# One queue to another: state-space tables issued by GpSimd, signed powers and a fourth raw weight buffer in a two-layer decoder trunk

## The chip, the core and the metric

The kernel runs on one core of one Trainium2 chip. The metric is device time in microseconds of one execution. A profiled execution also leaves a trace of every instruction on the five engines: TensorE (PE in the profile, its weight loads PEld), VectorE (DVE), ScalarE (ACT), GpSimd (POOL) and SyncE (SP), which here only issues DMAs. An engine runs its instructions in a fixed order: one that waits holds up all behind it. SPq and POOLq are the DMA issues of SyncE and GpSimd.

## The reference

An input x of 512 rows by 1024 passes through two layers, each x + norm(mixer(norm(x))), all in fp32. Layer 0 has two parallel branches, of which the first is the state-space layer that the change is about:

```python
# layer 0
p = u @ ev_w_in            # 1024 -> 5 x 1024: a_in, a_z, b_val, b_gate, b_z
lam_bar = exp(lam * dt)    # 64 groups, 64 complex states each
b_bar   = ((lam_bar - 1) / lam) * B
s_t     = lam_bar * s_{t-1} + b_bar @ u_t       # 16 channels per group
ya      = Re(C @ s_t) + D * u_t
ya      = glu(gelu(ya)) * silu(a_z)
yb      = pointwise(swish(layer_norm(conv31(b_val * sigmoid(b_gate))))) * silu(b_z)
x       = x + norm(concat(ya, yb) @ ev_w_out)
# layer 1: chunked gated linear attention, 4 heads, then out projection
```

## The kernel before

**Weights.** Every weight is cut into blocks of 128x1024 and used in the order of `wlist` (line 85): blocks 0 to 7 project to the state-space input, then four for each of eight channel blocks c (value, gate and two gates for the end), then the later layers. A block is loaded by SyncE into a raw tile (`w_raw`, line 113; three buffers `wraw`). fp32 products are made of a rounded high half and the remainder: ScalarE casts the high half `wh` (line 143). For most blocks the low half `wl` is made by ScalarE writing -raw, rounded, into `wl` (line 130) and a DMA issued by GpSimd that adds raw onto it (line 131); for the others VectorE subtracts (line 149). `mm_st` (line 181) then does 16 matmuls with the high half (lines 186, 187) and 8 with the low half (line 189).

**State-space parameters.** `s5_params` (line 308) computes on VectorE, on tiles of 128x64, the phase of lam_bar, the powers `pr` (eight powers and a one, real and imaginary), and `prb` (the powers times (lam_bar-1)/lam). GpSimd computes `wb`, powers of the unit phase (lines 416 to 424). These use scratch pools `s5w` and `nat0`, which are closed at lines 463 and 464, after which the pools `q5` and `h5` are opened on the same side of the memory.

**State-space blocks.** For each of eight blocks of eight groups, `s5_prep(c)` (line 513) loads the coefficients `cb` (line 519, two buffers). ScalarE makes a signed copy of C's real part in `csp` (line 522) and the negation of its imaginary part in `ci` (line 523). Outer products with the powers (`outer`, line 525) give `bmt`, on VectorE for c below 2 and on GpSimd after, and `cme`, on VectorE. TensorE transposes `bmt` (line 544) and multiplies it with `csp` (line 551); ScalarE copies that to `ks` (line 554), TensorE transposes `ks` (line 555), and VectorE adds D into `kt` (line 557). `kt` goes to a DRAM table padded with zeros, `kt_d`, and comes back as `tm` (lines 563, 565). `phases` (line 492) multiplies two levels of `wb` on GpSimd to the cosine and sine tables of a pair of blocks, and SyncE copies them to `ct` and `st` in four DMAs a block (line 573). `s5_in(c)` (line 579) does the input side and the scan, `s5_out(c)` (line 619) the output side: its first step multiplies `tm` and `cme` (line 628) and copies to `ys`, its second transposes and applies GELU.

**The main loop** (line 703) writes for each block c: the two steps of `s5_in(c+1)`, the five of `s5_prep(c+2)` and the two of `s5_out(c)`, interleaved by hand, then the value and gate projections with the convolution (`value_gate`, line 668; the convolution's 30 steps of line 655 have low priority), then two more projections (`gate_z`). After the loop come the half-GLU (line 734), the output projection's first half, the layer norm over channels (line 759), the pointwise projection and the rest.

**Order.** The program is written for a framework that plans the order itself (`schedule_with_timeline_sim=True`, line 1213): it puts each engine's instructions in an order by a model of their times, from priorities (`feed` raises, `background` lowers them) and from when a buffer comes free. The order in the text of the program is therefore not the order on an engine. PSUM tiles come from three rings of banks: `mm` (3), `cv` (2) and `aux` (3).

Of the kernel before, what the change touches and what calls it, by code (L numbers as in the profile page):

```python
# [9 lines left out]
F32 = mybir.dt.float32  # L10
# [3 lines left out]
ALU = mybir.AluOpType  # L14
# [3 lines left out]
P = 128  # L18
D = 1024
S = 512  # L20
KT = D // P
# [3 lines left out]
NG = 64  # L25
GP = 16
NS = 64
GC = P // GP
NB = 64
DVE_PREP = 2  # L30
TB = S // NB
# [20 lines left out]
def trunk(ctx: ExitStack, tc: tile.TileContext, A: dict, out: bass.AP, dbg: dict | None = None):  # L52
    nc = tc.nc
    V, G, SC, PE, SY = nc.vector, nc.gpsimd, nc.scalar, nc.tensor, nc.sync
# [4 lines left out]
    wpool = ctx.enter_context(tc.tile_pool(name="wpool", bufs=2, side="left"))  # L59
# [20 lines left out]
    sgn = const.tile([P, 1], F32, name="sgn")  # L80
# [32 lines left out]
    def w_raw():  # L113
        i = wst["next_raw"]
        if i >= len(wlist):
            return
        raw = wpool.tile([P, 1024], F32, tag="wraw", bufs=3, name=f"wraw{i}")
        SY.dma_start(raw, wlist[i])
        wst["raw"][i] = raw
        wst["next_raw"] = i + 1  # L120
# [147 lines left out]
    wb = s5p.tile([P, 2, 2, NG // 2, 8], F32, name="wb")  # L268
    decay = s5p.tile([P, NG], F32, name="decay")
    dg = s5p.tile([P, NG, GP], F32, name="dg")  # L270
    SW = ExitStack()
    sw = SW.enter_context(tc.tile_pool(name="s5w", bufs=1, side="right"))
    par = sw.tile([P, 3, NG], F32, name="s5par")
# [14 lines left out]
    SY.dma_start(dd, bass.AP(tensor=sd.tensor, offset=sd.offset, ap=[[NG, GP], [0, TB], [1, NG]]))  # L288
    w_raw()
    SY.dma_start(cw, A["conv_w"])  # L290

    tps = [ps("mm") for _ in range(3)] + [ps("cv") for _ in range(2)] + [ps("aux") for _ in range(3)]
    for tt in range(TT):
# [14 lines left out]
    def s5_params():  # L308
# [74 lines left out]
        tt_(t1, cp_, sq, ALU.mult)  # L383
        tt_(s1, s1, t1, ALU.add)


        V.memset(pr[:, 0, :, 8], 1.0)
        V.memset(pr[:, 1, :, 8], 0.0)
        V.tensor_tensor(out=pr[:, :, :, 7], in0=ph[:, :, :, 0], in1=e.unsqueeze(1).to_broadcast([P, 2, NG]), op=ALU.mult)

        scr = {V: [sw.tile([P, 2, NG, 4], F32, name=f"s5u{i}") for i in range(2)],
               G: [ya[:, i, 0:S // 2].rearrange("p (w g m) -> p w g m", w=2, m=4) for i in range(2)]}

        def cmul(eng, o, a, b):

            sh = list(a.shape)
            u, w = (x[:, :, :, :sh[3]] for x in scr[eng])
            eng.tensor_tensor(out=u, in0=a, in1=b[:, 0].unsqueeze(1).to_broadcast(sh), op=ALU.mult)
            eng.tensor_tensor(out=w, in0=a, in1=b[:, 1].unsqueeze(1).to_broadcast(sh), op=ALU.mult)
            eng.tensor_tensor(out=o[:, 0], in0=u[:, 0], in1=w[:, 1], op=ALU.subtract)  # L400
            eng.tensor_tensor(out=o[:, 1], in0=u[:, 1], in1=w[:, 0], op=ALU.add)

        for m in (1, 2, 4):
            lo = 8 - m
            cmul(V, pr[:, :, :, lo - m:lo], pr[:, :, :, lo:8], pr[:, :, :, lo:lo + 1])
# [3 lines left out]
        tt_(e2, e, e, ALU.mult)  # L409
        tt_(e2, e2, e2, ALU.mult)  # L410
        tt_(decay, e2, e2, ALU.mult)
        phs, ph2, ph4 = (sw.tile([P, 2, NG // 2, 1], F32, name=f"s5ph{i}") for i in (1, 2, 4))
        for a, rows in enumerate((slice(0, NS), slice(NS, P))):
            V.tensor_copy(phs[rows].rearrange("p w (i g) o -> p w i (g o)", g=GC),
                          ph[rows].rearrange("p w (i a g) o -> p w i a (g o)", a=2, g=GC)[:, :, :, a, :])
        cmul(G, ph2, phs, phs)
        cmul(G, ph4, ph2, ph2)
        for lvl in range(2):
            G.memset(wb[:, lvl, 0, :, 0], 1.0)
            G.memset(wb[:, lvl, 1, :, 0], 0.0)  # L420
# [32 lines left out]
        for o, (f0, f1, op) in enumerate(((cr, ci, ALU.subtract), (cis, crs, ALU.add))):  # L453
            V.tensor_tensor(out=prb[:, o], in0=pr[:, 0, :, 1:9], in1=bc(f0), op=ALU.mult)
            V.tensor_tensor(out=pt, in0=pr[:, 1, :, 1:9], in1=bc(f1), op=ALU.mult)
            V.tensor_tensor(out=prb[:, o], in0=prb[:, o], in1=pt, op=op)

        G.memset(md, 0.0)
        G.affine_select(out=md, in_=md, pattern=[[-TB, GP]], compare_op=ALU.not_equal, fill=1.0, base=1 - TB, channel_multiplier=1)
        G.tensor_tensor(out=dg, in0=md.unsqueeze(1).to_broadcast([P, NG, GP]), in1=dd.unsqueeze(2).to_broadcast([P, NG, GP]), op=ALU.mult)  # L460
# [2 lines left out]
    NP.close()  # L463
    SW.close()
    q5 = S5.enter_context(tc.tile_pool(name="q5", bufs=1, side="right", reuse_waits="tile"))
    h5 = S5.enter_context(tc.tile_pool(name="h5", bufs=2, side="right", reuse_waits="tile"))

    dump("u0h", uh.bitcast(F32))


    u_d = [dram.tile([P, TB, NB], F32, name=f"u_d{c}") for c in range(KT)]

    kt_d = [dram.tile([GP, 2 * TB - 1, P], F32, name=f"kt_d{i}") for i in range(2)]
    zt = q5.tile([P, (TB - 1) * P // TB], F32, name="zt")
    G.memset(zt, 0.0)
    for t in kt_d:
        SY.dma_start(t[:, TB:2 * TB - 1].rearrange("p s n -> p (s n)").rearrange("p (a b) -> p a b", a=TB), zt)

    csps = [q5.tile([P, GC, 32], F32, name=f"csp{i}") for i in range(2)]
    for t in csps:  # L480
        G.memset(t[:, :, GP:32], 0.0)

    svs = [q5.tile([P, GC, NB], F32, name=f"sv{i}") for i in range(2)]
    rv = q5.tile([P, GC, NB], F32, name="rv")
    for t in svs + [rv]:
        G.memset(t[:, :, 0:1], 0.0)

    prep = {}

    pair = {}  # L490

    def phases(c):

        sh = [P, GC, 8, 8]
        ws = slice(c // 2 * GC, c // 2 * GC + GC)

        def w1(w):
            return wb[:, 1, w, ws, :].unsqueeze(3).to_broadcast(sh)

        def w0(w):  # L500
            return wb[:, 0, w, ws, :].unsqueeze(2).to_broadcast(sh)

        out_ = []
        for o, (a, b, op) in enumerate(((0, 1, ALU.subtract), (1, 0, ALU.add))):
            r_ = h5.tile(sh, F32, tag=f"ph{o}", bufs=1, name=f"ph{o}_{c}")
            wt = h5.tile(sh, F32, tag="wt", bufs=1, name=f"wt{o}_{c}")
            G.tensor_tensor(out=r_, in0=w1(0), in1=w0(a), op=ALU.mult)
            G.tensor_tensor(out=wt, in0=w1(1), in1=w0(b), op=ALU.mult)
            G.tensor_tensor(out=r_, in0=r_, in1=wt, op=op)
            out_.append(r_.rearrange("p g a b -> p (g a b)"))  # L510
        pair[c // 2] = out_

    def s5_prep(c):

# [1 line left out]
        pe_ = V if c < DVE_PREP else G  # L516
        gs = slice(g0_, g0_ + GC)
        cb = h5.tile([P, 4, GC, GP], F32, tag="cb", bufs=2, name=f"cb{c}")
        SY.dma_start(cb, A["s5cb"][c])
        cr_ = csps[c % 2]  # L520
        ci_ = h5.tile([P, GC, GP], F32, tag="ci", bufs=1, name=f"ci{c}")
        SC.activation(cr_[:, :, 0:GP], cb[:, 0], AF.Copy, scale=sgn)
        SC.mul(ci_, cb[:, 1], -1.0)

        def outer(eng, o, pt, h, pw, m1, m2, pa):
            sh = list(o.shape)
# [5 lines left out]
            eng.tensor_tensor(out=o, in0=o, in1=pt, op=ALU.add)  # L532

        bm = q5.tile([P, GC, P], F32, tag="bm", bufs=2, name=f"bm{c}")
        cme = q5.tile([P, GC, TB, GP], F32, tag="cme", bufs=3, name=f"cme{c}")
        kt = q5.tile([P, GC, GP], F32, tag="kt", bufs=2, name=f"kt{c}")
        for h in range(2):
            hs = slice(h * 4, h * 4 + 4)
            bmt = q5.tile([P, 4, GP, TB], F32, tag="bmt", bufs=2, name=f"bmt{c}")
            pt1 = h5.tile([P, 4, GP, TB], F32, tag="wt", bufs=1, name=f"pt1_{c}")  # L540
            outer(pe_, bmt, pt1, h, prb, cb[:, 2, hs], cb[:, 3, hs], 2)
            tp = ps("aux")
            for j in range(4):
                PE.transpose(tp[:, j * P:(j + 1) * P], bmt[:, j].rearrange("p q s -> p (q s)"), ident)
            with feed():
                SC.copy(bm[:, hs, :], tp.rearrange("p (g n) -> p g n", n=P))
            yield

            kp = ps("aux")
            for j in range(4):  # L550
                PE.matmul(kp[32 * j:32 * j + 32, 0:P], cr_[:, h * 4 + j, :], bmt[:, j].rearrange("p q s -> p (q s)"), start=True, stop=True)
            ks = q5.tile([P, P], F32, tag="ks", bufs=2, name=f"ks{c}")
            with feed():
                SC.copy(ks, kp[:, 0:P])
            PE.transpose(kp[:, P:2 * P], ks, ident)
            with feed():
                V.tensor_tensor(out=kt[:, hs, :], in0=kp[:, P:2 * P].rearrange("p (g q) -> p g q", q=32)[:, :, 0:GP],
                                in1=dg[:, g0_ + h * 4:g0_ + h * 4 + 4, :], op=ALU.add)
            pt2 = q5.tile([P, 4, TB, GP], F32, tag="pt", bufs=1, name=f"pt2_{c}")
            outer(V, cme[:, hs], pt2, h, pr, cr_[:, hs, 0:GP], ci_[:, hs], 3)  # L560
            yield
        kd = kt_d[c % 2]
        SY.dma_start(kd[:, 0:TB], kt.rearrange("p g q -> p (g q)"))
# [3 lines left out]
        if c % 2 == 0:  # L567
            phases(c)
        half = slice(c % 2 * NS, c % 2 * NS + NS)
        ct_, st_ = (h5.tile([P, S], F32, tag=n, bufs=2, name=f"{n}{c}") for n in ("ct", "st"))  # L570
        for dst, src in zip((ct_, st_), pair[c // 2]):
            for r_ in range(2):
                SY.dma_start(dst[r_ * NS:r_ * NS + NS], src[half])
        prep[c] = (bm, cme, tm, ct_, st_)
        yield

# [119 lines left out]
    def run(g, n=1):  # L696
        for _ in range(n):
            next(g)
# [4 lines left out]
    for c in range(KT):  # L703
        nx = s5_in(c + 1) if c + 1 < KT else iter([None] * 2)
        pre = s5_prep(c + 2) if c + 2 < KT else iter([None] * 5)
        cur = s5_out(c)
        run(nx)
        run(pre, 2)
        run(nx)
        run(cur)  # L710
        run(pre, 2)
        run(cur)
        run(pre)
        value_gate(c)
        gate_z(zb_d[c])
        gate_z(za_d[c])
# [500 lines left out]
```

## Time and profile before

| | us |
|---|---|
| median of 3 runs | 946.44 |
| lowest, highest | 945.23, 946.85 |
| the profiled execution | 946.38 |
| its span, first to last instruction | 944.7 |
| TensorE busy | 897.7 |
| VectorE busy | 641.9 |
| ScalarE busy | 485.1 |
| GpSimd busy | 245.4 |
| mean granted TensorE clock | 0.981 of full |

In a row of a timeline stand the start and the length in us, the engine, the line, the operation, the output and the inputs; in brackets, the idle time of the engine before it and what ended that. Rows of one kind that follow each other are merged (x4). In the list of waits stand the waiting and the releasing instruction, the us in total, the number of waits and the longest. In a row of a group stand the busy us, the mean ns of one, and the idle us ahead of them. In a row of DMA issues stand the KB of each and the median us from issue to landing.

### The profile page before, as it was taken

The page shows a single profiled execution, that of the slowest core. Times are in us where ns is not written, and L with a number is a line of the kernel's source. Part 1 is how long each engine was busy: PE and PEld are TensorE (multiplying, and loading weights), DVE is VectorE, ACT ScalarE, POOL GpSimd, SP SyncE. Part 2 cuts the span into 40 slices and gives each one's busy share as a digit, 9 for nine tenths or more (in the row PEclk, how much of TensorE's full clock was granted, in tenths as well). Part 3 has the DMA queues.
Part 4 walks back from the last instruction along what each step waited for, and adds up shares of the span by engine and source line. Part 5 has one row for each costly group of instructions (what it writes and reads, how often), then busy time and mean ns, then how long its engine had stood idle before and what let it go on. Part 6 is the DMA issues. An engine that isn't in the chain of part 4 may idle for free. (4 is left out here: it accounts for less than half of the span.)

```text
span 944.7 us, 12134 instructions
## 1 busy us (share of the span) xinstructions
PE 897.7 (95%) x4396; PEld 718.9 (76%) x4396; DVE 641.9 (68%) x1206; ACT 485.1 (51%) x693; POOL 245.4 (26%) x258
## 2 busy tenths in 40 slices
PE   5995998999999999999999979999999999999996
PEld 4873776777778877778887758888888888888875
DVE  7953999999989989832579477584483232744546
ACT  6542786786678855564444566343543242523430
POOL 2693657463123422011054002000200020000222
PEclk8998999999999999999999979999999999999998
DMA  9877987787988885288463112212212223324412
GB/s 278 228 198 194 229 199 184 178 205 204 215 220 228 210 231 179 92 224 201 153 215 124 45 63 93 84 37 82 90 67 90 73 83 135 134 89 164 193 45 89
DMA packets 54955, 142.74 MB, mean 151 GB/s; under 512 B 14256, under 2 KB 15792, under 8 KB 54896
## 3 DMA queue, kind: packets, MB, share of 16 engines
q1 hardware_dynamic: 46832, 112.62, 35.9%
q0 software_dynamic: 8064, 29.36, 17.3%
q8 instruction: 34, 0.56, 0.2%
q14 instruction: 25, 0.20, 0.1%
HBM read 95.18 MB, written 13.22 MB: 115 GB/s over the span
## 5 line engine op out<-in xcount | busy, mean ns | idle before, releaser
L143 ACT CAST wh<-wraw 128x1024 fp32r<-128x1024 f32 x126 | 132.1, 1048 | 161.4 <-PE ps_mm L801 92.5
L149 DVE TENSOR_TENSOR wl<-wraw,wh 128x1024 fp32r<-128x1024 f32 x70 | 87.0, 1243 | 115.2 <-ACT wh L143 114.8
L655 DVE SCALAR_TENSOR_TENSOR ps_cv<-h,cw,ps_cv 128x512 f32<-128x512 f32 x232 | 161.7, 745 | 2.7 <-ACT ps_cv L652 1.8
L186 PE MATMUL ps_mm<-u0h,wh 128*128 128x512 f32 x320 | 129.9, 407 | 1.0 <-ACT tmp L679 0.7
L187 PE MATMUL ps_mm<-u0l,wh 128*128 128x512 f32 x320 | 129.4, 405 | 0.0
L800 PE MATMUL ps_mm<-wh,u1h 128*128 128x512 f32 x240 | 96.2, 402 | 3.5 <-ACT wh L143 3.4
L801 PE MATMUL ps_mm<-wh,u1l 128*128 128x512 f32 x240 | 96.3, 401 | 0.8 <-DVE u1l L194 0.8
L131 POOL DMA_DIRECT2D wl<-wraw x56 | 48.9, 884 | 182.4 <-ACT wl L130 178.2
L802 PE MATMUL ps_mm<-wl,u1h 128*128 128x512 f32 x240 | 91.6, 401 | 1.6 <-DVE wl L149 1.6
L189 PE MATMUL ps_mm<-u0h,wl 128*128 128x512 f32 x320 | 82.5, 395 | 1.1 <-DMA wl<-wraw 1.1
L186 PEld LDWEIGHTS ps_mm<-u0h,wh 128*128 128x128 f32 x320 | 61.8, 193 | 16.4 <-issue 1.6
L130 ACT ACTIVATE wl<-wraw 128x1024 fp32r<-128x1024 f32 x56 | 59.2, 1057 | 25.8 <-DMA wraw<-in_w_in_dram 14.0
L187 PEld LDWEIGHTS ps_mm<-u0l,wh 128*128 128x128 f32 x320 | 61.7, 193 | 13.9 <-issue 1.1
L189 PEld LDWEIGHTS ps_mm<-u0h,wl 128*128 128x128 f32 x320 | 59.4, 188 | 14.9 <-DMA wl<-wraw 1.5
L800 PEld LDWEIGHTS ps_mm<-wh,u1h 128*128 128x128 f32 x240 | 45.9, 191 | 14.9 <-ACT wh L143 3.8
L971 POOL TENSOR_TENSOR rg<-rg,ng 128x512 f32<-128x512 f32 x16 | 24.2, 1544 | 124.6 <-ACT rg L970 124.6
L802 PEld LDWEIGHTS ps_mm<-wl,u1h 128*128 128x128 f32 x240 | 45.6, 191 | 13.1 <-DVE wl L149 2.3
L801 PEld LDWEIGHTS ps_mm<-wh,u1l 128*128 128x128 f32 x240 | 45.9, 191 | 11.7 <-DVE u1l L194 1.2
L186 PE MATMUL ps_mm<-u1h,wh 128*128 128x512 f32 x128 | 50.7, 396 | 0.0
L187 PE MATMUL ps_mm<-u1l,wh 128*128 128x512 f32 x128 | 50.5, 394 | 0.0
L1062 POOL TENSOR_TENSOR kr<-kr,fac 128x384 f32<-128x384 f32 x8 | 6.7, 837 | 124.2 <-DVE rr L205 65.1
L800 PE MATMUL ps_mm<-wh,oth 128*128 128x512 f32 x96 | 37.8, 396 | 0.5 <-ACT wh L143 0.5
(341 smaller groups left out, 1993.6 us busy)
## 6 DMA issues: line engine op xcount, KB each, us to landing
wl<-wraw POOLq DMA_DIRECT2D x56, 512.0 KB, 6.1
wraw<-in_w_in_dram SPq DMA_DIRECT2D x40, 512.0 KB, 5.2
wraw<-in_w_out_dram SPq DMA_DIRECT2D x32, 512.0 KB, 3.3
wraw<-in_w_vr_dram SPq DMA_DIRECT2D x32, 512.0 KB, 3.2
wraw<-in_w_qk_dram SPq DMA_DIRECT2D x16, 512.0 KB, 3.3
tm<-kt_d SPq DMA_DIRECT2D x8, 512.0 KB, 6.3
wraw<-in_w_glu_dram SPq DMA_DIRECT2D x8, 512.0 KB, 5.8
wraw<-in_w_pw_dram SPq DMA_DIRECT2D x8, 512.0 KB, 5.1
```

The lines of the kernel that those rows point to most:

```text
L130: SC.activation(l, raw, AF.Copy, scale=-1.0)
L131: G.dma_start(l.bitcast(F32), raw, accum_op=ALU.add)
L143: SC.copy(h, raw)
L149: V.tensor_tensor(out=l, in0=raw, in1=h.bitcast(F32), op=ALU.subtract)
L186: PE.matmul(acc, whv[:, k, :], xh[:, k, :], start=(k == 0), stop=False)
L187: PE.matmul(acc, whv[:, k, :], xl[:, k, :], start=False, stop=False)
L189: PE.matmul(acc, wlv[:, k, :], xh[:, k, :], start=False, stop=(k == KT - 1))
L655: V.scalar_tensor_tensor(out=acc, in0=h[:, k:k + S], scalar=cw[:, c, k:k + 1], in1=acc, op0=ALU.mult, op1=ALU.add)
L800: PE.matmul(accs[tt], xh[:, kt, ts_], whj, start=(first and j == 0), stop=False)
L801: PE.matmul(accs[tt], xl[:, kt, ts_], whj, start=False, stop=False)
L802: PE.matmul(accs[tt], xh[:, kt, ts_], wlj, start=False, stop=(last and j == 1))
L971: G.tensor_tensor(out=r_, in0=r_, in1=ng, op=ALU.mult)
```

## The change

- *Signed powers.* After `prb` is made, the powers `pr` are multiplied in place, the real part by the sign column `sgn`, the imaginary part by -1. `cme` is then made from `cb` directly, and the tile `ci` and line 523 are gone. `csp` stays for the matmuls.
- *Queues.* The cosine and sine tables share a tile `cs`, copied in two DMAs a block in place of four, issued by GpSimd in place of SyncE. The loads of `cb` for c of 2 and more are issued by GpSimd too.
- *Fourth raw buffer.* Of the first 36 blocks, those with i % 4 == 3 are loaded into a tile of the pool `q5` with one buffer of its own.
- *Zero-fills first.* The zeros for `kt_d`, `csp`, `sv` and `rv` are written ahead of the parameters, in tiles of the pool `s5p`; the zero tile `zt` is filled by VectorE instead of GpSimd; the two DMAs of zeros stand behind the load of the convolution's weights.
- *Early squares.* `phs`, `ph2` and `ph4` stand ahead of the powers in the program.
- *Order and buffers.* The first step of `s5_out(c)` stands first in its round and the second step moves up; `cme` has two buffers in place of three, `bmt` three in place of two.

```diff
@@ w_raw
-        raw = wpool.tile([P, 1024], F32, tag="wraw", bufs=3, name=f"wraw{i}")
+        if i < 36 and i % 4 == 3:
+            raw = wst["pool"].tile([P, 1024], F32, tag="wraw", bufs=1, name=f"wraw{i}")
+        else:
+            raw = wpool.tile([P, 1024], F32, tag="wraw", bufs=3, name=f"wraw{i}")
         SY.dma_start(raw, wlist[i])
@@ ahead of the parameters, in s5p instead of q5
+    zt = s5p.tile([P, (TB - 1) * P // TB], F32, name="zt")
+    V.memset(zt, 0.0)
+    csps = [s5p.tile([P, GC, 32], F32, name=f"csp{i}") for i in range(2)]
+    for t in csps:
+        G.memset(t[:, :, GP:32], 0.0)
+    svs = [s5p.tile([P, GC, NB], F32, name=f"sv{i}") for i in range(2)]
+    rv = s5p.tile([P, GC, NB], F32, name="rv")
+    for t in svs + [rv]:
+        G.memset(t[:, :, 0:1], 0.0)
...
     SY.dma_start(cw, A["conv_w"])
+    for t in kt_d:
+        SY.dma_start(t[:, TB:2 * TB - 1].rearrange("p s n -> p (s n)").rearrange("p (a b) -> p a b", a=TB), zt)
@@ s5_params: phs, ph2, ph4 now stand ahead of the powers; after prb:
+        V.tensor_scalar(out=pr[:, 0], in0=pr[:, 0], scalar1=sgn, scalar2=None, op0=ALU.mult)
+        V.tensor_scalar(out=pr[:, 1], in0=pr[:, 1], scalar1=-1.0, scalar2=None, op0=ALU.mult)
@@ phases
-            r_ = h5.tile(sh, F32, tag=f"ph{o}", bufs=1, name=f"ph{o}_{c}")
+        cs = h5.tile([P, 2, GC, 8, 8], F32, tag="ph", bufs=1, name=f"ph{c}")
...
-        pair[c // 2] = out_
+        pair[c // 2] = cs.rearrange("p w g a b -> p w (g a b)")
@@ s5_prep
-        SY.dma_start(cb, A["s5cb"][c])
+        (SY if c < 2 else G).dma_start(cb, A["s5cb"][c])
         cr_ = csps[c % 2]
-        ci_ = h5.tile([P, GC, GP], F32, tag="ci", bufs=1, name=f"ci{c}")
         SC.activation(cr_[:, :, 0:GP], cb[:, 0], AF.Copy, scale=sgn)
-        SC.mul(ci_, cb[:, 1], -1.0)
...
-        cme = q5.tile([P, GC, TB, GP], F32, tag="cme", bufs=3, name=f"cme{c}")
+        cme = q5.tile([P, GC, TB, GP], F32, tag="cme", bufs=2, name=f"cme{c}")
...
-            bmt = q5.tile([P, 4, GP, TB], F32, tag="bmt", bufs=2, name=f"bmt{c}")
+            bmt = q5.tile([P, 4, GP, TB], F32, tag="bmt", bufs=3, name=f"bmt{c}")
...
-            outer(V, cme[:, hs], pt2, h, pr, cr_[:, hs, 0:GP], ci_[:, hs], 3)
+            outer(V, cme[:, hs], pt2, h, pr, cb[:, 0, hs], cb[:, 1, hs], 3)
...
-        ct_, st_ = (h5.tile([P, S], F32, tag=n, bufs=2, name=f"{n}{c}") for n in ("ct", "st"))
-        for dst, src in zip((ct_, st_), pair[c // 2]):
-            for r_ in range(2):
-                SY.dma_start(dst[r_ * NS:r_ * NS + NS], src[half])
+        cs = h5.tile([P, 2, S], F32, tag="cs", bufs=2, name=f"cs{c}")
+        for r_ in range(2):
+            G.dma_start(cs[r_ * NS:r_ * NS + NS], pair[c // 2][half])
+        ct_, st_ = cs[:, 0], cs[:, 1]
@@ main loop
         cur = s5_out(c)
+        run(cur)
         run(nx)
         run(pre, 2)
         run(nx)
         run(cur)
         run(pre, 2)
-        run(cur)
         run(pre)
```

More of the change, by code (lines that the diff above doesn't have):

```diff
@@ L270, in trunk @@
     dg = s5p.tile([P, NG, GP], F32, name="dg")
+    u_d = [dram.tile([P, TB, NB], F32, name=f"u_d{c}") for c in range(KT)]
+    kt_d = [dram.tile([GP, 2 * TB - 1, P], F32, name=f"kt_d{i}") for i in range(2)]
+    zt = s5p.tile([P, (TB - 1) * P // TB], F32, name="zt")
[7 more added lines that the diff above has]
+        G.memset(t[:, :, 0:1], 0.0)
     SW = ExitStack()
@@ L384, in s5_params @@
         tt_(s1, s1, t1, ALU.add)
-        V.memset(pr[:, 0, :, 8], 1.0)
-        V.memset(pr[:, 1, :, 8], 0.0)
-        V.tensor_tensor(out=pr[:, :, :, 7], in0=ph[:, :, :, 0], in1=e.unsqueeze(1).to_broadcast([P, 2, NG]), op=ALU.mult)
         scr = {V: [sw.tile([P, 2, NG, 4], F32, name=f"s5u{i}") for i in range(2)],
@@ L401, in cmul @@
             eng.tensor_tensor(out=o[:, 1], in0=u[:, 1], in1=w[:, 0], op=ALU.add)
+        phs, ph2, ph4 = (sw.tile([P, 2, NG // 2, 1], F32, name=f"s5ph{i}") for i in (1, 2, 4))
+        for a, rows in enumerate((slice(0, NS), slice(NS, P))):
+            V.tensor_copy(phs[rows].rearrange("p w (i g) o -> p w i (g o)", g=GC),
+                          ph[rows].rearrange("p w (i a g) o -> p w i a (g o)", a=2, g=GC)[:, :, :, a, :])
+        cmul(G, ph2, phs, phs)
+        cmul(G, ph4, ph2, ph2)
+        V.memset(pr[:, 0, :, 8], 1.0)
+        V.memset(pr[:, 1, :, 8], 0.0)
+        V.tensor_tensor(out=pr[:, :, :, 7], in0=ph[:, :, :, 0], in1=e.unsqueeze(1).to_broadcast([P, 2, NG]), op=ALU.mult)
         for m in (1, 2, 4):
@@ L411, in s5_params @@
         tt_(decay, e2, e2, ALU.mult)
[L412 to L417, printed above, removed]
         for lvl in range(2):
@@ L465, in trunk @@
     q5 = S5.enter_context(tc.tile_pool(name="q5", bufs=1, side="right", reuse_waits="tile"))
+    wst["pool"] = q5
     h5 = S5.enter_context(tc.tile_pool(name="h5", bufs=2, side="right", reuse_waits="tile"))
     dump("u0h", uh.bitcast(F32))
[L471 to L486, printed above, removed]
     prep = {}
@@ L501, in w0 @@
             return wb[:, 0, w, ws, :].unsqueeze(2).to_broadcast(sh)
-        out_ = []
+        cs = h5.tile([P, 2, GC, 8, 8], F32, tag="ph", bufs=1, name=f"ph{c}")
         for o, (a, b, op) in enumerate(((0, 1, ALU.subtract), (1, 0, ALU.add))):
-            r_ = h5.tile(sh, F32, tag=f"ph{o}", bufs=1, name=f"ph{o}_{c}")
             wt = h5.tile(sh, F32, tag="wt", bufs=1, name=f"wt{o}_{c}")
-            G.tensor_tensor(out=r_, in0=w1(0), in1=w0(a), op=ALU.mult)
+            G.tensor_tensor(out=cs[:, o], in0=w1(0), in1=w0(a), op=ALU.mult)
             G.tensor_tensor(out=wt, in0=w1(1), in1=w0(b), op=ALU.mult)
-            G.tensor_tensor(out=r_, in0=r_, in1=wt, op=op)
-            out_.append(r_.rearrange("p g a b -> p (g a b)"))
-        pair[c // 2] = out_
+            G.tensor_tensor(out=cs[:, o], in0=cs[:, o], in1=wt, op=op)
+        pair[c // 2] = cs.rearrange("p w g a b -> p w (g a b)")
     def s5_prep(c):
```

## The prediction, made before the changed kernel was timed

> **What bounds the kernel now.** The page comes first: the span, TensorE's share of it, and the span in 40 slices.
>
> ```profile
> span 944.7 us, 12134 instructions
> PE 897.7 (95%) x4396; PEld 718.9 (76%) x4396; DVE 641.9 (68%) x1206; ACT 485.1 (51%) x693; POOL 245.4 (26%) x258
> PE   5995998999999999999999979999999999999996
> DVE  7953999999989989832579477584483232744546
> ```
>
> TensorE works in 897.7 of 944.7 us, so only the other 47 us can be won by moving work about, and only where TensorE stands still. Past the start, slice 3 (71 to 94 us) is the one slice at 5. VectorE is at 8 or more from slice 4 to slice 15 and is the second bound to watch. The list of waits of TensorE names the places.
>
> ```profile
> PE ps_aux L555 <- ACT ks L554: 10.4, 1, 10.4
> PE ps_aux L551 <- DVE kt L557: 4.2, 3, 1.8
> PE ps_aux L588 <- DMA u<-u_d: 1.7, 1, 1.7
> ```
>
> The first row is one wait of 10.4 us, all of slice 3's hole; the hole at the very start is the normalising of x, which the change doesn't touch. The timelines around it, of TensorE, ScalarE, SyncE's queue and GpSimd in this order, tell who held whom.
>
> ```profile
> 81.94 0.41 PE L551 MATMUL ps_aux<-bmt,csp 128*32 128x128 f32 x4
> 92.74 0.48 PE L555 MATMUL ps_aux<-ident,ks 128*128 128x128 f32 x1 [10.38 <-ACT ks L554]
> ...
> 81.22 1.06 ACT L130 ACTIVATE wl<-wraw 128x1024 fp32r<-128x1024 f32 x1 [8.01 <-DMA wraw<-in_w_in_dram]
> 91.28 0.31 ACT L523 ACTIVATE ci<-cb 128x128 f32<-128x128 f32 x1 [8.99 <-DMA cb<-in_s5cb_dram]
> 91.49 1.03 ACT L143 CAST wh<-wraw 128x1024 fp32r<-128x1024 f32 x1
> 92.43 0.26 ACT L554 COPY ks<-ps_aux 128x128 f32<-128x128 f32 x1
> ...
> 69.82 5.10 SPq L573 DMA_DIRECT2D st<-ph  x4
> 75.64 10.08 SPq L118 DMA_DIRECT2D wraw<-in_w_in_dram  x3
> 85.81 0.58 SPq L519 DMA_DIRECT2D cb<-in_s5cb_dram  x1
> ...
> 68.83 0.87 POOL L131 DMA_DIRECT2D wl<-wraw  x1
> 75.45 1.37 POOL L507 TENSOR_TENSOR ph<-wb 128x512 f32<-128x512 f32 x1 [5.75 <-DMA ct<-ph]
> 76.77 0.86 POOL L131 DMA_DIRECT2D wl<-wraw  x1
> ```
>
> Read backwards: TensorE waits for a copy of 0.26 us (L554). In ScalarE's order that copy stands behind the negation of C's imaginary part (L523), which stands 8.99 us because the coefficients cb of block 3 are not there. Their DMA leaves SyncE's queue only at 85.81, behind three raw weight loads that take from 75.64 to 85.72, and these stood behind the eight table copies (L573; the last four are shown). So one wait at the head of two queues costs 10.38 us. Afterwards TensorE runs at half clock for a while; the table by stage gives it:
>
> ```profile
> 92.70:96.10 3.40, 3.36 (x10) 1.87 (x10) 0.69 (x1) 3.37 (x5) 0.00 (x0) 0.51 0.70 235
> 94.00:361.00 267.00, 259.26 (x1522) 203.32 (x1523) 253.97 (x366) 190.74 (x256) 112.78 (x98) 0.99 0.84 211
> 180.00:185.00 5.00, 4.66 (x20) 3.56 (x21) 5.00 (x10) 3.37 (x6) 3.13 (x4) 0.66 1.02 218
> ```
>
> The columns are the length, the busy time of TensorE, its weight loads, VectorE, ScalarE and GpSimd, then granted clock, DMA share and GB/s. From 92.70 to 96.10 the clock is 0.51: 3.40 x 0.49 = 1.7 us of work lost on top.
>
> **Signed powers.** L523 goes, with its waits; VectorE now takes both parts of C from cb, and the signs sit in the powers. That removes the instruction that held ScalarE. The other reader of cb on ScalarE, the signed copy for the matmuls (L522), stays, but it can't come before the last matmul that read the older contents, and the trace has it behind ks:
>
> ```profile
> 96.63 0.26 ACT L554 COPY ks<-ps_aux 128x128 f32<-128x128 f32 x1
> 96.78 0.40 ACT L522 ACTIVATE csp<-cb,sgn 128x128 f32<-128x128 f32 x1
> ```
>
> So I take the 10.38 us as gone, and the 1.7 us of half clock with them. What would be late next on ScalarE is L130: it ended at 82.28, and the cast (1.03) and ks (0.26) behind it would release TensorE at 83.57 instead of 82.35. That rest of 1.2 us goes too if its raw weight comes earlier, which the next part gives. Added are two scalings of 128x576 on VectorE; the normalising multiply of 128x512 stands for them.
>
> ```profile
> 7.18 0.49 DVE L297 TENSOR_SCALAR x<-x,rr 128x512 f32<-128x512 f32 x1
> 35.40 0.39 PE L186 MATMUL ps_mm<-u0h,wh 128*128 128x512 f32 x1
> 39.06 1.99 PE L189 MATMUL ps_mm<-u0h,wl 128*128 128x512 f32 x8
> 79.79 0.39 PE L186 MATMUL ps_mm<-u0h,wh 128*128 128x512 f32 x1
> ```
>
> Two of them are 2 x 0.49 x 576/512 = 1.1 us, about 42 us into the span, while TensorE is on the input projections (weight 3 starts at 35.40, weight 10 at 79.79). Nothing there waits for VectorE; without that cover they would cost 1.1 us.
>
> **Queues and the fourth raw buffer.** Sixteen merged table copies and six of the cb loads go from SyncE to GpSimd. SyncE is rid of the eight table copies between 66 and 75 us, and the raw loads behind them move up; with four buffers a raw load waits for a weight one tile older. I count ScalarE's 8.01 us wait for the raw weight as gone, and with it the 1.2 us rest. GpSimd pays:
>
> ```profile
> L131 POOL DMA_DIRECT2D wl<-wraw x27 | 23.5, 869 | 82.8 <-ACT wl L130 81.5 <-PE ps_mm L189 1.3
> wl<-wraw POOLq DMA_DIRECT2D x5, 512.0 KB, 5.3
> st<-ph SPq DMA_DIRECT2D x16, 128.0 KB, 4.4
> ```
>
> One DMA costs GpSimd 0.869 us, so 22 more are 19.1 us. From 94 to 361 it is busy for 112.78 of 267 us, so in sum there is room, but the order matters: the low halves of the weights (L131) stand in the same queue. Weight 10's is issued at 76.77 and lands 5.3 us later (the median of that window), at 82.1. TensorE wants it after weight 10's 16 matmuls with the high half. Weight 3 took 35.40 to 39.06 for these, 0.229 us each, so from 79.79 that is at 83.45: a slack of 1.4 us. In the new order the four table copies of the first pair take 4 x 0.87 = 3.5 us after 69.70, to 73.2, and land 4.4 us later, at 77.6; only then may the next tables overwrite the source, where now that is at 75.45. The low half behind slips by 2.1 us, 0.8 us past its slack. The bounds are 0, if the planner puts the low half first, and, if the four copies and the next two cb loads are all issued ahead of it, 6 x 0.87 - 1.4 = 3.8 us. I take 0.8, because the wait of 5.75 us that now stands ahead of L507 is where the copies fit.
>
> Here the Trainium skill speaks against the change: "DMA: Bandwidth & Descriptors", section "SWDGE vs HWDGE vs iDMA", gives plain transfers to SyncE or ScalarE, since GpSimd writes its descriptors into SBUF, from which VectorE can lock it out in its two-port modes. No lengthening shows in the 869 ns above, taken while VectorE was nearly always busy. By the rule the copies would cost more than my 0.8; its case is the first rival below.
>
> **Zero-fills, early square, order, buffers.** The fills of the padded tables move from about 48 us to the start. SyncE issues two small DMAs more before weight 2's load.
>
> ```profile
> 7.00 0.33 SPq L118 DMA_DIRECT2D wraw<-in_w_in_dram  x1
> 47.91 0.58 SPq L477 DMA_DIRECT2D kt_d<-zt  x1
> 47.69 0.19 POOL L475 MEMSET zt<- 128x112 f32 x1
> 2.00 0.43 POOL L676 MEMSET h<- 128x30 f32 x6
> ```
>
> Two at 0.58 us hold that load from 7.00 to 8.2; weight 2 isn't multiplied until after weight 1, so I cost this at nothing (1.2 us at most if that cover fails). The squares of the unit phase start before the powers; GpSimd's chain has no reader on TensorE before the tables: nothing, or a gain inside the term above. The output half of a block now leads its round, which lets cme do with two buffers, and bmt has three. This bears on the waits for kt (4.2 us) and u (1.7 us). VectorE's order decides these, and it is full either way; I take 0, between a gain of all 5.9 us and a loss of the same size.
>
> **Does the gain reach the end?** The convolution fills VectorE and must end before the layer norm.
>
> ```profile
> 91.62 0.69 DVE L530 TENSOR_TENSOR pt<-pr,ci 128x512 f32<-128x512 f32 x1 [14.03 <-ACT ci L523]
> 96.73 0.76 DVE L655 SCALAR_TENSOR_TENSOR ps_cv<-h,cw,ps_cv 128x512 f32<-128x512 f32 x1 [0.93 <-ACT ps_cv L652]
> 408.91 0.69 DVE L194 TENSOR_TENSOR xbl<-ln,xbh 128x512 fp32r<-128x512 f32 x1 [2.35 <-ACT xbh L193]
> 413.00 0.47 PE L186 MATMUL ps_mm<-xbh,wh 128*128 128x512 f32 x1 [0.88 <-ACT wh L143]
> ```
>
> VectorE works 253.97 of the 267 us from 94 to 361, so it can't catch up 12 us there. It need not: it stood for 14.03 us by the same instruction L523, and its first convolution step (96.73) follows the same gate, so both engines start earlier together. At the far end the last normalised tile is ready at 409.6, while TensorE wants it as the eighth of eight, 14 matmuls of 0.229 us after 413.00, at 416.2: 6.6 us of slack. So all of the gain passes.
>
> The sum, on the profiled execution's 946.38 us (span 944.7, and 1.7 around it; the median of the three is 946.44): 946.38 - 10.38 - 1.7 + 0.8 = 935.1; I say 935.0. Its own range, from the bounds above, is 929 to 939.
>
> **Rivals.** *GpSimd's queue gives part of it back.* Copies stand ahead of low halves in every block. For it: the slack of 1.4 us, and the copy's wait for the consumers of its buffers stops everything behind it. Against it: 82.8 us of GpSimd's idle time ahead of L131. Price: 3.8 at the first pair instead of 0.8, and a like 3 us once more in the blocks after: 935 + 3 + 3 = 941. The Trainium skill's rule on plain transfers would end here too. *More goes than I count.* The kt and u waits (5.9) vanish too, with the half clock around 180 (5.00 x 0.34 = 1.7): 935 - 7.6 = 927. The row of 180 to 185 follows waits of under 2 us. The Trainium skill ("TensorE: Matmul & The Clock Gate", section "Why this matters for your kernels") has the clock drop only for gaps over about 3 us; by it the 1.7 would not go with them and this case gives 929; the row contradicts that. *Slower: the fourth buffer opens late.* It is carved from the pool q5, which takes the room of the parameter scratch. The first touch of that pool in the trace is the fill at 47.69, though a fill that stands later in the program ran at 2.00; so something holds the pool back. Weight 3 is the first to use the buffer. Loaded from 47.69 it would land 5.2 later (the page's median for these loads), be cast 1.05 later and meet TensorE at 53.9 instead of 35.40: 18.5 lost, 12 won, 953.
>
> ```profile
> wraw<-in_w_in_dram SPq DMA_DIRECT2D x40, 512.0 KB, 5.2
> ```
>
> It decides if TensorE keeps the weights' order and the load leaves after about 41 us; against it, the planner can take weights 4 to 6 first. *The wait only changes its name.* If cb of block 3 leaves GpSimd as late as it left SyncE and some other reader of it stands ahead of ks, ScalarE stops as before: 946. Against it stand the two rows of L554 and L522.
>
> **Chances.** Forecast 0.50, queue 0.15, more 0.13, renamed wait 0.10, late buffer 0.12. A measurement of this kernel can tell about 0.2%, 1.9 us, from no change. Faster: 0.50 + 0.15 + 0.13 = 0.78; same 0.10; slower 0.12. The range 924 to 946 leaves out the late buffer (0.12), half of the renamed wait (0.05) and a little below.
>
> **What would show it.** Right: no wait of L555 for ks over 1 us; TensorE at 9 in slice 3; no L523; the raw loads issued before 75 us; the first L655 near 85 us; the stages past 420 us as long as now. The queue rival shows as TensorE waits for wl by DMA between 80 and 280 us, the late buffer as a hole at weight 3 between 35 and 55 us. The forecast is wrong if the time is above 940, or if the hole goes and the waits for kt grow by as much.

## The result, and the profile after

The changed kernel takes 958.06 us (median of 4 runs, 957.3 to 962.38) against 945.84 us (4 runs, 943.94 to 946.85) for the kernel before on the same chip: a ratio of the means of 1.0141, 95% interval 1.0106 to 1.0176. It is 1.4% slower; 935.0 was forecast. The profiled execution took 957.3 us, its span is 955.6. Most line numbers of the changed kernel are 4 to 7 higher than before (L186 is L190, L519 is L526, L555 is L560, L655 is L660). The page first:

```profile
span 955.6 us, 12092 instructions
PE 901.7 (94%) x4396; PEld 721.7 (76%) x4396; DVE 657.3 (69%) x1209; ACT 484.8 (51%) x686; POOL 259.1 (27%) x279
PE   5669998999999899999999979999999999999996
DVE  7980699999999999852469576585483322744546
```

A slice is now 23.9 us. The old hole in slice 3 is gone: TensorE is at 9 there. In its stead slices 1 and 2 (24 to 72 us), which were at 9, are at 6, and slice 13 (311 to 334 us) fell from 9 to 8. The list of waits of TensorE names what is new; the figures are us in total, times, longest:

```profile
PE ps_mm L193 <- DMA wl<-wraw: 7.2, 3, 4.4
PE ps_mm L190 <- ACT wh L147: 6.5, 1, 6.5
PE ps_aux L549 <- DVE bmt L537: 5.3, 1, 5.3
...
PE ps_mm L190 <- DVE h L685: 3.2, 1, 3.2
```

No wait of L560 for ks is left. The timelines show three holes in a row, with the queues that made them: TensorE, then SyncE, ScalarE, VectorE and GpSimd.

```profile
41.12 0.80 PE L190 MATMUL ps_mm<-u0h,wh 128*128 128x512 f32 x1 [6.48 <-ACT wh L147]
52.36 1.12 PE L549 MATMUL ps_aux<-ident,bmt 128*128 128x128 f32 x4 [5.33 <-DVE bmt L537]
59.21 3.35 PE L193 MATMUL ps_mm<-u0h,wl 128*128 128x512 f32 x7 [4.44 <-DMA wl<-wraw]
...
18.04 9.31 SPq L122 DMA_DIRECT2D wraw<-in_w_in_dram  x3
...
35.29 0.33 SPq L671 DMA_DIRECT2D u_d<-tmp  x1
35.67 0.42 SPq L122 DMA_DIRECT2D wraw<-in_w_in_dram  x1
...
34.68 0.58 ACT L670 COPY tmp<-ps_mm 128x512 f32<-128x512 f32 x1 [4.40 <-PE ps_mm L193]
39.08 1.06 ACT L134 ACTIVATE wl<-wraw 128x1024 fp32r<-128x1024 f32 x1 [3.81 <-DMA wraw<-in_w_in_dram]
...
51.47 0.83 DVE L537 TENSOR_TENSOR bmt<-bmt,pt 128x512 f32<-128x512 f32 x1
...
54.60 0.87 POOL L135 DMA_DIRECT2D wl<-wraw  x1
```

By the order of SyncE's queue in the compiled program, the three loads that start at 18.04 are those of weights 4, 5 and 6. The load of weight 3 leaves at 35.67, directly behind the store of input block 2 (L671), which waits for ScalarE's copy at 34.68, which waits for TensorE to finish weight 2. So the weight wanted next is fetched only when the one before it is used up. It is in ScalarE's hands at 39.08 and in TensorE's at 41.12. The other two holes follow from the orders that the planner wrote around that late weight: TensorE has the transposes of bmt (L549) behind weight 3's high half, ahead of its low half and of weight 4, and VectorE makes bmt only at 51.47; and GpSimd has weight 3's low half (L135) near the end of its chain of unit-phase products, at 54.60. Sum of the waits: 6.48 + 5.33 + 4.44 = 16.25 us. The clock comes on top, in the table by stage:

```profile
41.10:44.50 3.40, 3.38 (x8) 2.73 (x9) 3.37 (x5) 2.82 (x3) 3.24 (x6) 0.50 0.00 0
52.40:54.80 2.40, 2.37 (x7) 1.15 (x7) 2.40 (x3) 0.58 (x1) 2.32 (x4) 0.50 0.00 0
59.20:62.60 3.40, 3.39 (x8) 2.71 (x9) 3.33 (x3) 0.00 (x0) 3.40 (x4) 0.52 0.68 145
```

At clocks of 0.50, 0.50 and 0.52 these stretches lose 1.7 + 1.2 + 1.6 = 4.5 us. The loss of about 21 us eats the 12 that the old stall had cost, and more.

### The profile page after: what moved, and what is told of

Read it like the earlier page. It is cut to its first block, busy times and chain, and to the rows that moved or that the text cites. A ratio compares the mean times of both kernels' runs of the same rounds, so it can differ in the third digit from the quotient of the medians.

```text
span 955.6 us, 12092 instructions
## 1 busy us (share of the span) xinstructions
PE 901.7 (94%) x4396; PEld 721.7 (76%) x4396; DVE 657.3 (69%) x1209; ACT 484.8 (51%) x686; POOL 259.1 (27%) x279
## 4 chain that ended last, share of the span: by engine, by line
PE 68%; DVE 19%; DMA 5%; ACT 5%; issue 2%; POOL 1%; SPq 0%; DVEq 0%; ACTq 0%; POOLq 0%
PE ps_mm L193 10%; PE ps_mm L190 10%; PE ps_mm L191 10%; PE ps_mm L807 9%; PE ps_mm L805 9%; PE ps_mm L806 9%; DVE ps_cv L660 4%; PE ps_aux L1083 2%; DMA wl<-wraw 2%; DVE yal L198 1%; DVE cme L533 1%; DMA u<-u_d 1%; PE ps_aux L633 1%; DMA wraw<-in_w_out_dram 1%; PE ps_mm L899 1%
## 5 line engine op out<-in xcount | busy, mean ns | idle before, releaser
L660 DVE SCALAR_TENSOR_TENSOR ps_cv<-h,cw,ps_cv 128x512 f32<-128x512 f32 x232 | 163.3, 747 | 2.2 <-ACT ps_cv L657 1.3
L190 PE MATMUL ps_mm<-u0h,wh 128*128 128x512 f32 x320 | 129.9, 406 | 6.7 <-ACT wh L147 6.5
L135 POOL DMA_DIRECT2D wl<-wraw x56 | 50.4, 934 | 155.0 <-ACT wl L134 135.5
L190 PEld LDWEIGHTS ps_mm<-u0h,wh 128*128 128x128 f32 x320 | 61.1, 191 | 23.1 <-ACT wh L147 6.9
L190 PE MATMUL ps_mm<-u1h,wh 128*128 128x512 f32 x128 | 50.7, 396 | 0.0
```

What stands on the lines that cost most here:

```text
L135: G.dma_start(l.bitcast(F32), raw, accum_op=ALU.add)
L190: PE.matmul(acc, whv[:, k, :], xh[:, k, :], start=(k == 0), stop=False)
L660: V.scalar_tensor_tensor(out=acc, in0=h[:, k:k + S], scalar=cw[:, c, k:k + 1], in1=acc, op0=ALU.mult, op1=ALU.add)
```

## The experiments

The kernel before, timed beside these on the same chips, took 945.96 to 946.82 us. Times are medians; each ratio is of the means, to that kernel, with its 95% interval.

**Is it the fourth buffer, and is it its number or its place?** Theory A: the load stands in SyncE's queue where its pool opens. Four kernels. The first goes back to three buffers:

```
-        if i < 36 and i % 4 == 3:
-            raw = wst["pool"].tile([P, 1024], F32, tag="wraw", bufs=1, name=f"wraw{i}")
-        else:
-            raw = wpool.tile([P, 1024], F32, tag="wraw", bufs=3, name=f"wraw{i}")
+        raw = wpool.tile([P, 1024], F32, tag="wraw", bufs=3, name=f"wraw{i}")
```

> The changed kernel with three raw weight buffers for all weights, the rest of the change kept. Theory A (the load of weight 3 stands in SyncE's queue behind the store of input block 2, because its buffer belongs to a pool that opens late): the three holes of TensorE between 34 and 60 us (6.48, 5.33 and 4.43 us, together 16.2) go, and with them the low clock of that stretch; 932 to 940. Rival B (GpSimd's longer queue delays the low halves of the weights): the holes at low halves stay, since the queues are as in the changed kernel; 948 to 956. Rival C (VectorE falls behind because of the new order of the blocks, 3 to 6 us around 325): the late part of the loss stays, 940 to 948.

Measured: 950.54 us, ratio 1.0035 (1.0013 to 1.0057). The three holes go, as A says, but 950.5 is not 936: something else costs. The number lies in B's span, though not by B's mechanism: the waits for low halves come to 3.2 us. The longest wait was in no expectation:

```profile
PE ps_aux L629 <- DMA tm<-kt_d: 9.7, 1, 9.7
```

The second puts the fourth buffer alone into the kernel before (the branch above, the pool q5, and two buffers of cme instead of three for room).

> The kernel before with the fourth raw weight buffer alone, put where the change puts it; to make room for it the output matrices get two buffers instead of three. Theory A: the load of weight 3 leaves only after input block 2 is stored, TensorE waits for it as in the changed kernel, 15 to 20 us lost at 35 to 60; the old wait of 10.4 us for ks may stay or go, since everything ahead of it is late too: 950 to 966. Rival B (GpSimd's queue): the queues are the old ones, so 944 to 949.

Measured: 953.72 us, ratio 1.0084 (1.0057 to 1.0112), within A's span and outside B's: waits of 6.6 for wh, 6.7 for wl and 3.8 for bmt, at the old queues. Only 7.4 us are lost here, since the old wait of 10.4 us for ks is not in this kernel's list any more; presumably the late weight hides it. The third keeps four buffers and takes the fourth from the pool that is open from the start:

```
-    wst["pool"] = q5
+    wst["pool"] = s5p
```

> The changed kernel with the fourth raw buffer taken from the pool that is open from the start, nothing else altered. Theory A: not the number of buffers but the late opening costs; the load of weight 3 leaves before 12 us, no hole at weight 3; 930 to 940, like three buffers or up to 3 us better. If four buffers cost something by themselves (more transfers at once on the DMA engines): 945 to 958.

Measured: 949.73 us, ratio 1.0022 (1.0000 to 1.0044). The time alone would speak for "four buffers cost by themselves". But no wait of TensorE over 0.6 us is left between 14 and 60 us, the kernel equals the one with three buffers, and the same new wait for tm (8.5 us) is here too. So the place costs and not the number. The fourth kernel puts the late buffer onto a base without other faults (signed powers and GpSimd's queue, 938.17 below):

```
+        if i < 36 and i % 4 == 3:
+            raw = wst["pool"].tile([P, 1024], F32, tag="wraw", bufs=1, name=f"wraw{i}")
...
+    wst["pool"] = q5
...
-        cme = q5.tile([P, GC, TB, GP], F32, tag="cme", bufs=3, name=f"cme{c}")
+        cme = q5.tile([P, GC, TB, GP], F32, tag="cme", bufs=2, name=f"cme{c}")
```

> Signed powers and GpSimd's queue (938.2) with the fourth raw buffer where the change puts it, and two buffers of cme to make room. Theory A: the load of weight 3 stands behind the store of input block 2, holes at weight 3 as in the changed kernel: 8 to 16 us slower, 946 to 954. If the late buffer only costs together with the new order and the fills: 937 to 941.

Measured: 954.27 us, ratio 1.0078 (1.0052 to 1.0103): 16.1 us more than its base, and the same three waits.

```profile
PE ps_mm L193 <- DMA wl<-wraw: 6.7, 3, 4.3
PE ps_mm L190 <- ACT wh L147: 6.6, 1, 6.6
PE ps_aux L548 <- DVE bmt L536: 5.1, 1, 5.1
```

**Does the old stall go by the signed powers or by the queues?** Signed powers alone:

```
+        V.tensor_scalar(out=pr[:, 0], in0=pr[:, 0], scalar1=sgn, scalar2=None, op0=ALU.mult)
+        V.tensor_scalar(out=pr[:, 1], in0=pr[:, 1], scalar1=-1.0, scalar2=None, op0=ALU.mult)
...
-        SC.mul(ci_, cb[:, 1], -1.0)
...
-            outer(V, cme[:, hs], pt2, h, pr, cr_[:, hs, 0:GP], ci_[:, hs], 3)
+            outer(V, cme[:, hs], pt2, h, pr, cb[:, 0, hs], cb[:, 1, hs], 3)
```

> The kernel before with the signed powers alone: no negated copy of C on ScalarE. By the prediction's step the wait of 10.4 us for ks goes with the 1.7 us of half clock: 933 to 937. If the wait only changes its name, since the raw loads and the coefficients still stand behind the table copies in SyncE's queue: 943 to 948. In between (raw weight 1.2 us late on ScalarE): 936 to 940.

Measured: 943.26 us, ratio 0.9961 (0.9935 to 0.9987), at the lower end of the span given for a renamed wait (its ten runs reach from 935.29 to 947.43). The stall did partly change its name. The timeline of VectorE and TensorE:

```profile
86.77 0.77 DVE L531 TENSOR_TENSOR pt<-pr,cb 128x512 f32<-128x512 f32 x1 [12.19 <-DMA cb<-in_s5cb_dram]
87.46 0.21 DVE L558 TENSOR_TENSOR kt<-ps_aux,dg 128x64 f32<-128x64 f32 x1
...
87.72 0.64 PE L552 MATMUL ps_aux<-bmt,csp 128*32 128x128 f32 x2 [4.41 <-DVE kt L558]
```

VectorE reads cb itself now, stands 12.19 us for it, and kt, which TensorE needs, is queued behind: 4.41 us instead of 10.38. With the tables and the later coefficients on GpSimd's queue in addition, merged as in the change:

```
-        SY.dma_start(cb, A["s5cb"][c])
+        (SY if c < 2 else G).dma_start(cb, A["s5cb"][c])
...
-                SY.dma_start(dst[r_ * NS:r_ * NS + NS], src[half])
...
+            G.dma_start(cs[r_ * NS:r_ * NS + NS], pair[c // 2][half])
```

> The kernel before with signed powers and with the tables and later coefficients on GpSimd's queue, merged as in the change. Base: signed powers alone, 943.3. By the prediction's own terms 0.8 us more for weight 10's low half and 1.2 us less for its raw weight: 941 to 945. The queue rival of the prediction (copies ahead of low halves in every block): 946 to 951.

Measured: 938.17 us, ratio 0.9911 (0.9884 to 0.9938), better than either theory had it: cb no longer stands behind the raw loads, and the wait for kt is 0.9.

```profile
PE   5999989999999999999999979999999999999996
...
PE ps_aux L587 <- DMA u<-u_d: 3.6, 2, 3.2
PE ps_mm L186 <- ACT tmp L678: 3.4, 3, 1.6
PE ps_aux L543 <- DVE bmt L531: 2.0, 1, 2.0
...
PE ps_aux L550 <- DVE kt L556: 0.9, 1, 0.9
```

The queues were also put back by themselves, in the changed kernel with three raw buffers (both `G.dma_start` of the excerpt above to `SY`):

> The changed kernel with three raw buffers and with tables and coefficients back on SyncE's queue (the merged copies kept). Base: three raw buffers alone, 950.5. If GpSimd's queue is what costs: 940 to 946. If SyncE's queue is the one that holds up kt and tm (they stand behind raw loads already): the table copies join them there, tm is later still, 950 to 958.

Measured: 946.75 us, ratio 0.9994 (0.9968 to 1.0020), between the two. The wait for tm is as long there (9.4 us), so its length isn't GpSimd's doing. The intervals of this kernel and of its base (1.0013 to 1.0057) overlap; the 3.8 us between them are left unexplained.

**What is the wait for tm?** The block's transition matrices go from kt to DRAM and back as tm. The kernel with the early fourth buffer shows it on SyncE's queue and on TensorE:

```profile
84.37 0.33 SPq L122 DMA_DIRECT2D wraw<-in_w_in_dram  x1
84.79 0.56 SPq L568 DMA_DIRECT2D kt_d<-kt  x1
91.04 0.33 SPq L122 DMA_DIRECT2D wraw<-in_w_in_dram  x1
91.46 0.56 SPq L570 DMA_DIRECT2D tm<-kt_d  x1
...
99.96 0.70 PE L633 MATMUL ps_aux<-tm,u 128*64 128x128 f32 x4 [8.46 <-DMA tm<-kt_d]
```

The store of kt and the load of tm each stand behind a raw weight load. They did so before as well (tm left at 92.98), and TensorE did not wait, because the output half of a block came late in its round. The change puts it first, and with it the first matmul with tm: 272 weight matmuls stand ahead of it in TensorE's order, 292 with the old place. Theory D: this place is what costs. The old place, in that kernel:

```
         cur = s5_out(c)
-        run(cur)
         run(nx)
...
         run(pre, 2)
+        run(cur)
         run(pre)
```

> The changed kernel with the fourth raw buffer in the pool open from the start, and with the output halves back in their old place in the round. Theory D (the leading output half makes TensorE reach its first matmul with tm 20 matmuls, 4.6 us, earlier, before tm is back from DRAM): the wait of 8.5 us for tm goes or shrinks to under 4, with the low clock behind it; 938 to 943 against 949.7 with the new order. Rival (tm is late for another reason and something waits as long): 946 to 951.

Measured: 942.00 us, ratio 0.9942 (0.9920 to 0.9964); the wait for tm is gone and the time is 7.7 us less, as D has it. But the trace shows a wait as long elsewhere, as its rival has it:

```profile
PE ps_aux L593 <- DMA u<-u_d: 7.0, 1, 7.0
```

The waits for ks, za and sv shrink in exchange, from 6.9 us in sum to 0.2. So 7.7 us is what the new place costs in all; that the wait for tm is what makes it up is not shown. The new place alone, on signed powers, with the change's counts of cme and bmt:

> The kernel before with signed powers, and with the new place of the output halves and its buffer counts (two of cme, three of bmt). With signed powers alone it took 943.3, with the first use of tm at 105.0 and tm loaded from 91.4. Theory D: the first use comes 4.6 us earlier, at 100.4, and tm is there at about 99, so little or no wait: 942 to 946. If the order costs by itself wherever it stands (VectorE behind in the later blocks): 947 to 953.

Measured: 944.43 us, ratio 0.9991 (0.9968 to 1.0015), 1.2 us above its base, inside the spread. The time fits and the reasoning doesn't: a wait of 5.3 us for tm and three for ks (6.3 in sum) are new, and the waits of the base for kt (5.6 in sum, the 4.4 among them) are gone in exchange. And in the changed kernel as it is:

> The changed kernel, late fourth buffer and all, with the output halves in their old place. Its own trace has no wait for tm, since the late buffer makes TensorE reach that matmul only at 111.9. If the order costs only through that wait (theory D), it costs nothing here: 956 to 960, as the changed kernel. If the order costs 7.7 us everywhere, as it did with the buffer opened early: 948 to 952.

Measured: 959.25 us, ratio 1.0131 (1.0106 to 1.0157). The place costs nothing there, since the late weight makes TensorE reach the first tm only at 111.9 us. One wait hides the other.

**What happens after 311 us?** The change puts the zero-filled tables (csp, sv, rv) into s5p. In the compiled program they lie at bytes 221,152 to 229,344 of each partition, and the gates sz of the next stage take 212,960 to 229,344. Before, those bytes held the powers and other parameters. The tables are in use to the last block (sv to its output matmuls at 302.7 us), and the gates' first load leaves at 305.4. Loads of the gates, GpSimd's products with them, and VectorE's splits beside them; the changed kernel, and below it the kernel before:

```profile
L738 SPq DMA_DIRECT2D sz<-za_d x8: 320/488/1342, 305.4 to 337.8; - x8
...
312.14 8.14 POOL L746 TENSOR_TENSOR sz<-ya,sz 128x512 f32<-128x512 f32 x5 [8.89 <-DMA sz<-za_d]
...
317.99 6.24 DVE L198 TENSOR_TENSOR yal<-ya,yah 128x512 fp32r<-128x512 f32 x3
324.15 0.74 DVE L660 SCALAR_TENSOR_TENSOR ps_cv<-h,cw,ps_cv 128x512 f32<-128x512 f32 x1
...
329.34 0.68 DVE L685 TENSOR_TENSOR h<-ps_mm,tmp 128x512 f32<-128x512 f32 x1
...
L198 DVE TENSOR_TENSOR yal<-ya,yah 128x512 fp32r<-128x512 f32 x8 | 14.5, 1850 | 1.2 <-ACT yah L197 1.2
```

```profile
L733 SPq DMA_DIRECT2D sz<-za_d x8: 320/560/1072, 264.9 to 332.3; - x8
...
L194 DVE TENSOR_TENSOR yal<-ya,yah 128x512 fp32r<-128x512 f32 x8 | 5.6, 734 | 0.0
```

The gates' loads start 40 us later, five products run in one go, and a split of VectorE takes 1850 ns on average instead of 734. The splits take 8.9 us more in sum, the last h stands behind them, and TensorE waits 3.2 us for it. Theory E says this is the place of the tables. Three kernels: the fills of the change on the base of 938.17; a small pool of their own for tables and fourth buffer, on the base of 942.00; the same pool for the tables alone, in the changed kernel:

```
+    zp = S5.enter_context(tc.tile_pool(name="zp", bufs=1, side="right"))
...
-    csps = [s5p.tile([P, GC, 32], F32, name=f"csp{i}") for i in range(2)]
+    csps = [zp.tile([P, GC, 32], F32, name=f"csp{i}") for i in range(2)]
...
-    rv = s5p.tile([P, GC, NB], F32, name="rv")
+    rv = zp.tile([P, GC, NB], F32, name="rv")
```

> Signed powers and GpSimd's queue (938.2 by themselves) and the zero-filled tables moved to the start and into the long-lived pool, as in the change. Theory E: those tables are read until the last block of the state-space part, and the pool's bytes are the first that the next stage's gates reuse; so the gates are loaded after 294 us instead of from 258, GpSimd's gate products fall upon VectorE's splits, which take about 1.8 us instead of 0.73, and the last h comes late: 3 to 6 us slower, 941 to 945. Rival, the prediction's own term: the fills cost nothing, 936 to 940.

Measured: 942.28 us, ratio 0.9954 (0.9931 to 0.9977): 4.1 us more, splits at 1787 ns, gates loaded from 290.5, a wait of 2.6 us for the last h. This is a difference of medians: the profiled execution is the fastest of ten (937.67 to 945.84) and, slow splits and all, only 0.8 us above the profiled one of the base.

> The changed kernel with the old place of the output halves, and with the zero-filled tables and the fourth raw buffer in a small pool of their own, open from the start, whose bytes the next stage's gates don't take. Base: the same with both in the long-lived pool, 942.0. Theory E: the gates load early again, the splits take 0.73 us, TensorE's wait of 2.6 us for the last h goes: 936 to 940. If the slow splits have another cause: 941 to 943 with the splits still at 1.8 us.

Measured: 937.98 us, ratio 0.9892 (0.9854 to 0.9929): 4.0 us less, splits at 748 ns, gates from 258.8, no wait for the last h.

> The changed kernel with the zero-filled tables alone in a small pool of their own, whose bytes the next stage's gates don't take; the fourth raw buffer stays late. Theory E: about 4 us come back, as in the two runs on the other base: 952 to 956, with the splits at 0.73 us and no wait for the last h. If the loss after 320 us only follows from the late start: 957 to 960.

Measured: 953.99 us, ratio 1.0079 (1.0060 to 1.0098): 4.1 us less than the changed kernel, the gates loaded from 275.3 instead of 305.4, and the three early waits still there.

```profile
L739 SPq DMA_DIRECT2D sz<-za_d x8: 319/446/594, 275.3 to 338.5; - x8
...
L198 DVE TENSOR_TENSOR yal<-ya,yah 128x512 fp32r<-128x512 f32 x8 | 5.6, 739 | 0.0
```

Each step alone is near what a pair of these intervals can tell; three bases with the same sign and size, and the same rows in the trace, decide it.

**The early squares, and the good parts together.** The copies of the unit phase and its first two squares ahead of the powers, on the base of 938.17:

> Signed powers and GpSimd's queue (938.2) with the unit phase squared before the powers. The prediction costs it at nothing: 936 to 940. If VectorE's and GpSimd's early chains collide, or the tables come earlier: up to 3 us either way.

Measured: 936.33 us, ratio 0.9893 (0.9865 to 0.9922). 1.8 us less is inside the spread: no cost, perhaps a gain. To that the zero-fills at the start, in the pool zp:

> Signed powers, GpSimd's queue, early squares, and the zero-fills first in a pool of their own; three raw buffers, old order of the halves, old counts of cme and bmt. If the parts that proved good add up and the fills cost nothing by themselves: 934 to 938, as without the fills (936.3). If moving the fills costs by its DMAs and its reshuffled order: 939 to 943.

Measured: 937.01 us, ratio 0.9903 (0.9882 to 0.9923). The fills cost nothing by themselves once the tables lie elsewhere, and gain nothing. Four kernels lie together at 936 to 938, about 1% faster than the kernel before and over 2% faster than the changed one; that of 938.17 needs the least for it: signed powers and queues.

## Why the prediction was wrong, point by point

The ledger, from the kernel before: signed powers and queues 946.3 to 938.2 (-8.2); late fourth buffer +16.1; tables in the long-lived pool +4.1; squares -1.8; new place of the output halves 0 beside the late buffer. 938.2 + 16.1 + 4.1 - 1.8 = 956.6, against 958.1 measured.

*Signed powers, -10.38 and -1.7.* Right in place and sign. The sum with the queue's 0.8 came to -11.3, and 8.2 were measured. The credit went to the wrong part: without the queues VectorE waits for cb in ScalarE's stead, as the rival of the renamed wait had it, and 3.1 us are gained. In the kernel of 938.17 waits for u (3.6 against 1.7 before), tmp (3.4 against 0.7) and bmt (2.0 against none) give part back.

*Queue of GpSimd, +0.8, and its rival at 941.* On the base of signed powers the queue helped: 943.26 without, 938.17 with it, with intervals that just overlap. In the changed kernel with three raw buffers it went the other way (946.75 without, 950.54 with it), and that stays open. In the changed kernel TensorE's waits for a low half between 80 and 280 us come to one of 1.87 us. The Trainium skill's rule ("DMA: Bandwidth & Descriptors", section "SWDGE vs HWDGE vs iDMA") that plain transfers are better off on SyncE's or ScalarE's queue did not decide here. Its mechanism would lengthen the issue of a low half; the mean of 56 issues was 884 ns before, 891 in the kernel of 938.17 and 934 in the changed one.

*Fourth buffer, 0, with "late buffer" as a rival of 0.12.* This is the step that failed. The rival had the place (a hole at weight 3 between 35 and 55 us) and nearly the time (953), and a wrong reason and condition. The reason: the buffer does not lie in the room of the parameter scratch. In the compiled program it has bytes 160,544 to 164,640, and the scratch begins at 173,536; its load waits for no engine. But the planner opens the pool only when the parameters are planned, so in the list of instructions the load stands directly behind the first write into that pool, and in SyncE's queue behind everything planned earlier. The condition, a load later than 41 us, was not met (35.67), and by its arithmetic 35.67 would have cost only the first hole: 35.67 + 5.2 + 1.05 = 41.92, against 41.12 in the trace. The other two holes came from the orders of TensorE and GpSimd, which the planner had written around the late weight; the rival's price left them out. That 953 lies near 958 is therefore luck: it is 18.5 us lost in one hole less 12 won, where the runs show 16.1 for three holes and 4.1 for the tables, less 8.2 and 1.8 won. The prediction put the buffer at nothing for the reason that each raw load then waits for a weight one tile older; the first load into it is not held by a tile but by its place in the queue.

*Zero-fills, 0 (1.2 at most).* The cost was looked for where the fills went, at the start, and there was none. It was where the tables stay: 4.1 us, by bytes that the next stage wants.

*Order and buffers, 0 between -5.9 and +5.9.* 0 in the changed kernel, but by cover: 7.7 us when the fourth buffer opens early, more than the 5.9 allowed for.

*The sum's own range, 929 to 939.* Its bounds do not give this. The queue at 3.8, the 1.2 us rest of L130, the 1.2 of the fills and a loss of 5.9 in the waits make 946 at the top; 928 is the bottom.

*Does the gain reach the end.* From the last stretches nothing was lost: TensorE's slices from 14 on (334 us) show the digits of before.

*What would show it.* No wait for ks and a 9 in slice 3 came true, and did not make the kernel faster: they show that a stall is gone, not that nothing took its place. The sign that failed was the first convolution step, expected near 85 us: it came at 104.0 (96.7 before, 88.9 in the kernel of 938.17). The hole at weight 3, named as the late buffer's sign, was there too, in slices 1 and 2.

## What to carry to other kernels

A new buffer is only as early as its place in the queue: see what stands ahead of its load in the compiled order, since a free buffer whose pool opens late may be filled behind work that its own data has to feed. When a tile moves to another pool, ask which tile of the next stage gets those bytes and when the moved one is read last. And before a step that hides under a stall is booked at zero, price it with that stall removed.

## What the runs showed of the hardware

A subtraction of VectorE of two operands in SBUF takes 2.5 times as long (1850 against 734 ns) while GpSimd multiplies tiles in SBUF, and GpSimd's product 1666 ns at the median against 1298; VectorE's convolution steps in between, with one operand in PSUM, stay at 0.74 us. That agrees with the Trainium skill, "SBUF — State Buffer", section "Who interferes with whom": a VectorE instruction with two inputs in SBUF contends with a GpSimd instruction that reads SBUF, and the pair of ports that they share is an exclusive lock.

The granted clock after a short wait has no clean threshold here. In the kernel of 938.17, after waits of 1.97 us (74.89) and 1.62 us (194.68):

```profile
75.00:80.00 5.00, 5.00 (x18) 3.99 (x19) 1.90 (x4) 1.54 (x2) 0.00 (x0) 0.66 1.03 277
194.70:199.70 5.00, 5.00 (x22) 4.13 (x23) 5.00 (x9) 3.57 (x4) 3.58 (x6) 1.00 0.57 105
```

The sixth figure after the length, the clock, is 0.66 after the one and 1.00 after the other; before, a wait of 1.66 us was followed by 0.66. After waits of 4.4 to 10.4 us it was 0.50 to 0.52 in the 2.4 to 4 us looked at.
